# SwiGLU over 8192 rows: giving each partition a contiguous region of HBM of its own

## The chip, the cores and the metric

The kernel runs on one core of a Trainium2 chip. The metric is the device time of one execution in microseconds. Runs of one kernel are called fast or slow: a run over 1.5% above the fastest of the same kernel counts as slow, and ratios use fast runs alone.

## The reference

```python
x = np.random.randn(8192, 8192).astype(np.float32)

def reference(x):
    a, b = np.split(x, 2, axis=-1)
    silu_b = b / (1 + np.exp(-b))
    return a * silu_b
```

It reads 268.4 MB and writes 134.2 MB, and does two cheap operations per element.

## The kernel before

A tile is 128 partitions, each with two neighbouring rows of x (a "row pair", 64 KiB). Tile i takes row pairs 128 i to 128 i + 127, so a tile is one contiguous 8 MiB of HBM, and partition p lies 64 KiB after partition p - 1. Three buffers go round; SyncE issues loads, ScalarE issues stores, ScalarE computes silu and VectorE multiplies in place.

```python
    R = 2
    BUFS = 3
    xv = x.tensor.reshape([N // R, R * M]).ap()
    ov = out.tensor.reshape([N // R, R * half]).ap()
    ntiles = N // (P * R)          # 32
    ...
    def load(i, rows=None):
        ...
        nc.sync.dma_start(
            out=tiles[i][:, lo * M : hi * M], in_=xv[i * P : (i + 1) * P, lo * M : hi * M]
        )
    ...
    def store(i, c0=0, cw=R * half):
        (nc.scalar if i < last - 1 else nc.sync).dma_start(
            out=ov[i * P : (i + 1) * P, c0 : c0 + cw], in_=tiles[i][:, c0 : c0 + cw]
        )
```

Of the kernel before, what the change touches and what calls it, by code (L numbers as in the profile page):

```python
# [1 line left out]

# [4 lines left out]

_SILU = mybir.ActivationFunctionType.Silu


@with_exitstack
def kernel(
    ctx: ExitStack,
    tc: tile.TileContext,
    x: bass.AP,
    out: bass.AP,
):




    nc = tc.nc
    N, M = x.shape
    half = M // 2
    P = nc.NUM_PARTITIONS
    R = 2
    BUFS = 3

    xv = x.tensor.reshape([N // R, R * M]).ap()  # L30
    ov = out.tensor.reshape([N // R, R * half]).ap()
    ntiles = N // (P * R)
    last = ntiles - 1

    pool = ctx.enter_context(tc.tile_pool(name="sbuf", bufs=BUFS))
    ctx.enter_context(tc.manual_schedule())
    tiles = {}

    def load(i, rows=None):
        if i not in tiles:  # L40
            tiles[i] = pool.tile([P, R * M], x.dtype, name="xt")
        lo, hi = (0, R) if rows is None else rows
        nc.sync.dma_start(  # L43
            out=tiles[i][:, lo * M : hi * M], in_=xv[i * P : (i + 1) * P, lo * M : hi * M]
        )

    def swiglu(i, k, c0=0, cw=half):
        xt = tiles[i]
        b = xt[:, k * M + half + c0 : k * M + half + c0 + cw]
        nc.scalar.activation(out=b, in_=b, func=_SILU)  # L50
        nc.vector.tensor_mul(  # L51
            out=xt[:, k * half + c0 : k * half + c0 + cw],
            in0=xt[:, k * M + c0 : k * M + c0 + cw],
            in1=b,
        )

    def store(i, c0=0, cw=R * half):
        (nc.scalar if i < last - 1 else nc.sync).dma_start(
            out=ov[i * P : (i + 1) * P, c0 : c0 + cw], in_=tiles[i][:, c0 : c0 + cw]
        )  # L60

    for i in range(BUFS):
        load(i)
    for i in range(last):
        for k in range(R):
            swiglu(i, k)
        if i == last - 1:
            swiglu(last, 0)
        store(i)
        nxt = i + BUFS  # L70
        if nxt < last:
            load(nxt)
        elif nxt == last:
            load(last, (0, 1))
            load(last, (1, 2))

    store(last, 0, half)
    for c0 in range(0, half, half // 2):
        swiglu(last, 1, c0, half // 2)
    store(last, half, half)  # L80


# [1 line left out]
_INS = ['x']  # L84
_OUTS = [((8192, 4096), 'float32')]


# [23 lines left out]
```

## Time and profile before

| | before |
|---|---|
| time, median of 6 runs | 936.24 us (935.77 to 937.38) |
| span of the profiled run | 934.8 us |
| VectorE / ScalarE busy | 30% / 25% |
| packets on the DMA queues, share of 16 engines' span | 99.8% |
| steady rate | 434 GB/s |

A packet is one record of a DMA engine in the trace; a load is cut into 128 of them, one for the run of each partition. Three further lines of the page of before are of use later: the rate in 40 slices, and the issues with the median time from issue to landing at the end of the line.

```profile
GB/s 404 400 445 430 430 439 433 428 435 443 428 430 439 429 442 432 435 426 453 419 430 452 411 452 423 428 447 425 433 433 453 414 443 429 426 447 428 425 437 376
...
out_dram<-xt ACTq DMA_DIRECT2D x30, 4096.0 KB, 39.7
...
xt<-in_x_dram SPq DMA_DIRECT2D x31, 34.5
```

The reader is to see that from the third slice to the last but one the rate only wavers around 434 GB/s. A load of 8 MiB takes 34.5 us to land, and not the 19.3 us that eight packets per engine would take alone, because other transfers share the engines with it.

### The profile page before, as it was taken

The page shows a single profiled execution, that of the slowest core. Times are in us where ns is not written, and L with a number is a line of the kernel's source. Part 1 is how long each engine was busy: PE and PEld are TensorE (multiplying, and loading weights), DVE is VectorE, ACT ScalarE, POOL GpSimd, SP SyncE. Part 2 cuts the span into 40 slices and gives each one's busy share as a digit, 9 for nine tenths or more (in the row PEclk, how much of TensorE's full clock was granted, in tenths as well). Part 3 has the DMA queues.
Part 4 walks back from the last instruction along what each step waited for, and adds up shares of the span by engine and source line. Part 5 has one row for each costly group of instructions (what it writes and reads, how often), then busy time and mean ns, then how long its engine had stood idle before and what let it go on. Part 6 is the DMA issues. An engine that isn't in the chain of part 4 may idle for free.

```text
span 934.8 us, 367 instructions
## 1 busy us (share of the span) xinstructions
DVE 283.3 (30%) x65; ACT 229.4 (25%) x66; POOL 0.2 (0%) x4
## 2 busy tenths in 40 slices
DVE  0333312333123331133321333213332133331242
ACT  0223320233302333113331133311333203332041
POOL 0000000000000000000000000000000000000000
DMA  9999999999999999999999999999999999999998
GB/s 404 400 445 430 430 439 433 428 435 443 428 430 439 429 442 432 435 426 453 419 430 452 411 452 423 428 447 425 433 433 453 414 443 429 426 447 428 425 437 376
DMA packets 9506, 402.67 MB, mean 431 GB/s; under 512 B 1056, under 2 KB 1056, under 8 KB 1056
## 3 DMA queue, kind: packets, MB, share of 16 engines
q1 hardware_dynamic: 5184, 276.83, 68.6%
q10 hardware_dynamic: 4320, 125.83, 31.2%
q14 instruction: 2, 0.02, 0.0%
HBM read 268.44 MB, written 134.22 MB: 431 GB/s over the span
## 4 chain that ended last, share of the span: by engine, by line
DMA 84%; DVE 10%; ACT 4%; DVEq 0%; issue 0%; SPq 0%; ACTq 0%
DMA out_dram<-xt 42%; DMA xt<-in_x_dram 42%; DVE xt L51 10%; ACT xt L50 4%; DVEq L106 0%; SPq L43 0%; ACTq L50 0%; DVEq L51 0%
## 5 line engine op out<-in xcount | busy, mean ns | idle before, releaser
L51 DVE TENSOR_TENSOR xt<-xt 128x4096 f32<-128x4096 f32 (+1 forms) x65 | 283.3, 4359 | 637.7 <-ACT xt L50 634.5
L50 ACT ACTIVATE xt<-xt 128x4096 f32<-128x4096 f32 (+1 forms) x65 | 228.1, 3556 | 688.1 <-DMA xt<-in_x_dram 688.1
L50 ACT ACT_TABLE_LOAD x1 | 1.3, 1283 | 0.7 <-PEq L95 0.7
L95 POOL MEMSET const-bfloat16-1.0<- 128x1 bf16 x1 | 0.1, 103 | 0.0
L95 POOL MEMSET const-uint8-127<- 128x1 uint8 x1 | 0.1, 102 | 0.0
L95 POOL MEMSET const-float32-0.0<- 128x1 f32 x1 | 0.1, 100 | 0.2 <-issue 0.2
L95 POOL MEMSET const-float32-1.0<- 128x1 f32 x1 | 0.1, 99 | 0.0
## 6 DMA issues: line engine op xcount, KB each, us to landing
out_dram<-xt ACTq DMA_DIRECT2D x30, 4096.0 KB, 39.7
xt<-in_x_dram SPq DMA_DIRECT2D x2, 4096.0 KB, 27.1
out_dram<-xt SPq DMA_DIRECT2D x1, 4096.0 KB, 23.6
out_dram<-xt SPq DMA_DIRECT2D x2, 2048.0 KB, 14.5
xt<-in_x_dram SPq DMA_DIRECT2D x31, 34.5
```

The costliest lines, as they stand in the source:

```text
L50: nc.scalar.activation(out=b, in_=b, func=_SILU)
L51: nc.vector.tensor_mul(out=xt[:, k * half + c0 : k * half + c0 + cw], in0=xt[:, k * M + c0 : k * M + c0 + cw], in1=b,)
L95: nc = _bacc.Bacc("TRN2", target_bir_lowering=False, num_devices=1)
```

## The change

Its intent: each of 16 groups of 8 partitions works through a contiguous region of its own, 16 MiB of x and 8 MiB of out. Within a group every partition walks through its own 2 MiB of x, one row pair per tile.

```diff
-    xv = x.tensor.reshape([N // R, R * M]).ap()
-    ov = out.tensor.reshape([N // R, R * half]).ap()
     ntiles = N // (P * R)
+    G = 16
+    xv = x.rearrange("(e j i r) m -> i e j (r m)", i=ntiles, e=G, r=R)
+    ov = out.rearrange("(e j i r) m -> i e j (r m)", i=ntiles, e=G, r=R)
@@ load @@
-            out=tiles[i][:, lo * M : hi * M], in_=xv[i * P : (i + 1) * P, lo * M : hi * M]
+            out=tiles[i][:, lo * M : hi * M], in_=xv[i, :, :, lo * M : hi * M]
@@ store @@
-            out=ov[i * P : (i + 1) * P, c0 : c0 + cw], in_=tiles[i][:, c0 : c0 + cw]
+            out=ov[i, :, :, c0 : c0 + cw], in_=tiles[i][:, c0 : c0 + cw]
```

In the built program the pattern of a load is 128 runs of 16384 elements at a step of 524288 elements (2 MiB) instead of 16384 (64 KiB). The 16 x 8 of the source has folded into 128. This step from partition to partition is called the pitch below.

## The prediction

> **What bounds the kernel now.** I read the page's first two parts first, to see which engine is full:
>
> ```profile
> DVE 283.3 (30%) x65; ACT 229.4 (25%) x66; POOL 0.2 (0%) x4
> ...
> DMA  9999999999999999999999999999999999999998
> DMA packets 9506, 402.67 MB, mean 431 GB/s; under 512 B 1056, under 2 KB 1056, under 8 KB 1056
> ```
>
> VectorE and ScalarE are busy less than a third of the span of 934.8 us. The DMA row is at nine tenths or more in 39 of 40 slices. The small packets are 1056 semaphore writes of 4 bytes and carry nothing.
>
> Next the queues and the chain that ended last, to see what the transfers consist of and whether compute stands between them:
>
> ```profile
> q1 hardware_dynamic: 5184, 276.83, 68.6%
> q10 hardware_dynamic: 4320, 125.83, 31.2%
> ...
> DMA 84%; DVE 10%; ACT 4%; DVEq 0%; issue 0%; SPq 0%; ACTq 0%
> ```
>
> The two shares add to 99.8% of what 16 engines could do in the span, so there is practically no gap. The 14% of DVE and ACT in the chain are not gaps of the DMA either: while one tile is computed, the other two buffers of the ring load or store. The busy time by window confirms this; its columns are the window, its length, the busy time of DVE, ACT and POOL with counts, PEclk, the DMA share and GB/s:
>
> ```profile
> 0.00:12.00 12.00, 0.00 (x0) 1.28 (x1) 0.20 (x4) 1.00 0.86 350
> 12.00:46.00 34.00, 8.85 (x2) 7.12 (x2) 0.00 (x0) 1.00 1.03 427
> 46.00:75.00 29.00, 8.85 (x2) 7.12 (x2) 0.00 (x0) 1.00 1.00 434
> ...
> 400.00:487.00 87.00, 25.93 (x7) 20.75 (x7) 0.00 (x0) 1.00 1.00 434
> ...
> 900.00:935.00 35.00, 9.51 (x4) 7.33 (x3) 0.00 (x0) 1.00 0.91 393
> ```
>
> In the steady part the share is 1.00 and the rate 434 GB/s. Finally I read the single packet records of the trace. Of the 3968 packets of 65,536 bytes, median and ninth decile are both 2418 ns (27.1 GB/s per engine; times 16 that is 433.7 GB/s). The 3840 packets of 32,768 bytes on the store queue take 1213 ns, with a maximum of 1221 ns. Such constancy says that nothing behind the engines, HBM in particular, ever holds a packet up: the engine sets its own pace. All long packets but two fall into the first 55 us, where the queues start (3.0 to 3.5 us for the first ones, up to 4.1 us where stores first join loads).
>
> So the floor of this program is 402.65 MB / 434 GB/s = 928 us. The span is 935 us: 7 us of start and tail are all that could be won with the same bytes.
>
> **What the Trainium skill says.**
> 1. "DMA: Bandwidth & Descriptors", section "Where 436 GB/s comes from", puts the ceiling of 16 engines at 435.2 GB/s. The trace agrees: 434 in every steady window. "HBM Reference", section "Specifications (TRN2)", gives 716 GB/s for the memory that two cores share, so with one core running HBM has room above the 434 as long as its parts are evenly loaded. The equal packet times are consistent with that.
> 2. "DMA: Bandwidth & Descriptors", section "Latency and other measured facts", row "HBM row pitch at large powers of two", bears directly on the change. Copies of 128 partitions x 16 KiB between HBM tensors reached, per direction, 207 GB/s at a pitch of 512 KiB from partition to partition, 164 at 2 MiB, 103 at 4 and 8 MiB, and 214 again at 4 MiB padded by 4 KiB. The page calls channel aliasing of streams in lockstep an inference. The trace of before cannot test it: its pitches are only 64 KiB (loads) and 32 KiB (stores), and it shows no slow steady state there.
> 3. The same page, section "The descriptor swizzle", has 16 engines with 8 partitions each. The trace fits: an 8 MiB load is 128 packets of 64 KiB, eight per engine, 8 x 2.418 = 19.3 us.
>
> **The change part by part.** It removes and adds no instruction. In the built program the order on every engine is the same: 31 loads of 128 x 16384 elements, two half loads, 33 stores, 65 activations, 65 multiplications, the same three buffers and waits. The SBUF side is identical. The split of 128 partitions into 16 groups of 8 folds back into one step, because eight steps of 2 MiB make exactly 16 MiB. What is left is this:
> - A load's partition step in x goes from 64 KiB to 2 MiB; the run within a partition stays 64 KiB (32 KiB in the halves of the last tile).
> - A store's partition step in out goes from 32 KiB to 1 MiB; the run stays 32 KiB.
> - From tile to tile the loads move 64 KiB instead of 8 MiB.
>
> A. Descriptors and issue: same counts and sizes, hence 0 us.
> B. ScalarE and VectorE: same shapes, 65 x 3.51 us and 65 x 4.36 us, both under a third of the span; 0 us.
> C. Locality: every partition walks through its own 2 MiB. This could only save something if HBM held the engines up now, and constant 2418 ns say it does not. At most a few us at the start; I count 0.
> D. Pitch, loads: the 16 engines now start at addresses that differ by multiples of 8 or 16 MiB, all advancing from the same offset. The page's 2 MiB figure is 164 / 214 = 0.77 of full. Estimate: 434 x 0.77 = 333 GB/s, so 268.4 MB take 806 us instead of 618 us: +188 us.
> E. Pitch, stores: 1 MiB lies between the page's 512 KiB (207 / 214 = 0.97) and 2 MiB (0.77). With 0.86 the rate is 373 GB/s and 134.2 MB take 360 us instead of 309 us: +51 us.
>
> The DMA is the path that sets the end, so D and E lie wholly on it: 936 + 188 + 51 = 1175 us if the page's ratios carry over in full. They may not. The page's copies both read and write HBM in each packet, with both sides at the bad pitch; here each packet has HBM on one side and SBUF on the other. Its row was 16 KiB and here it is 64 or 32 KiB, so an engine running 20 us ahead is on another partition and others may slip past it. And one core at 434 GB/s leaves headroom below 716. I take about 60% of the 239 us: 936 + 144 = 1080 us.
>
> **Rivals.**
> 1. The pitch does nothing: the headroom absorbs uneven load, or the engines fall out of step and stay so. For: in the first 4 us of before the sixteen first packets start within 0.8 us of each other, take up to 3.47 us, and from the second packet on nearly all take 2418 ns, with starts spread over only 0.6 us. A small offset is enough there. Against: those were 64 KiB steps, where different address bits differ. Result: 933 to 940 us.
> 2. Locality is worth something, and the larger regions help. For: a change of this intent. Against: the engines are at their own pace, floor 928 us. Result: 930 us at best, which is less than 2%.
> 3. Both sides alias in full: all 402.65 MB at 333 GB/s is 1209 us plus 7 for start and tail, 1216 us. The limit could even apply per direction: 268.4 MB at 164 GB/s would be 1637 us, which I hold for unlikely because then the loads would have to run at less than half of an engine's pace.
> 4. Waits take over: if loads slow down and stores do not, the loads' queue is the longer one, and ScalarE waits for it as it does now (688 us of its 935 us waiting). Three buffers are then just as short as before; no new bound, but the idle of both engines grows with the span.
>
> **Range and chances.** The outcomes have two humps: near 936 (rivals 1 and 2, some 38%) and a broad one from 1000 to 1240 (D and E in part or whole, some 60%). The range from 932 to 1240 takes in both; the rest lies above. The point, 1080, is a compromise weighted to the second hump. Faster by over 2% would need under 918 us, below the floor of 928: 1%. Within 2%: 38%. Slower: 61%.
>
> **What would show it.** If D holds, the 64 KiB packets of the load queue take more than 2418 ns throughout and scatter (3150 ns at the page's ratio), the steady windows keep a DMA share near 1.00 but fall from 434 to between 330 and 400 GB/s, and ACT's wait for loads grows. E shows in 32 KiB packets of the store queue longer than 1213 ns, less so than the loads (1.16 times against 1.30 times). A and B hold if packet counts and the means of 3.5 and 4.4 us stand. Rival 1 shows as 2418 and 1213 ns unchanged. The prediction is wrong in its main step if packet times are unchanged, or if only one of the two queues slows while the other keeps its time; and it is wrong in size if packets take over 1.4 times as long.

## The result, and the profile after

The changed kernel takes 997.83 us (median of 6 runs, 995.75 to 1004.92) against 936.24 us: slower, ratio 1.0668, 95% interval 1.0635 to 1.0701. A ratio here is the mean time of one kernel's fast runs over that of the other's fast runs in the same rounds, so it is not quite the ratio of the medians quoted. The result is correct.

From the page of the changed kernel, the lines that answer to those of before:

```profile
DVE 283.3 (28%) x65; ACT 229.4 (23%) x66; POOL 0.2 (0%) x4
...
DMA  9999999999999999999999999999999999999995
GB/s 350 374 386 405 413 425 421 414 428 404 416 422 407 429 416 426 411 421 416 409 433 414 409 401 412 417 405 407 404 392 389 388 421 403 392 405 411 404 418 251
DMA packets 9506, 402.67 MB, mean 404 GB/s; under 512 B 1056, under 2 KB 1056, under 8 KB 1056
...
q1 hardware_dynamic: 5184, 276.83, 68.9%
q10 hardware_dynamic: 4320, 125.83, 29.7%
...
DMA 82%; DVE 10%; ACT 4%; another core or an unknown queue 1%; issue 0%; DVEq 0%; ACTq 0%; SPq 0%
...
out_dram<-xt ACTq DMA_DIRECT2D x30, 4096.0 KB, 40.8
...
xt<-in_x_dram SPq DMA_DIRECT2D x31, 38.4
```

Packet counts, bytes and compute times are those of before. The engines are still full (98.6% of 16 spans), but they move 404 GB/s instead of 431. So the packets themselves became longer. Loads land 3.9 us later, stores 1.1 us. (The 1% of "another core or an unknown queue" is mostly one wait of 13.5 us near the start that the profile could not assign.)

The windows of the changed kernel (columns as in the prediction: window, length, DVE, ACT and POOL busy with counts, PEclk, DMA share, GB/s):

```profile
0.00:12.00 12.00, 0.00 (x0) 1.28 (x1) 0.20 (x4) 1.00 0.97 350
12.00:46.00 34.00, 8.85 (x2) 7.12 (x2) 0.00 (x0) 1.00 0.98 369
46.00:75.00 29.00, 8.85 (x2) 7.12 (x2) 0.00 (x0) 1.00 1.01 386
75.00:104.00 29.00, 8.85 (x2) 7.12 (x2) 0.00 (x0) 1.00 0.98 398
104.00:133.00 29.00, 8.85 (x2) 7.12 (x2) 0.00 (x0) 1.00 1.01 424
400.00:487.00 87.00, 23.11 (x6) 20.08 (x6) 0.00 (x0) 1.00 1.01 418
487.00:574.00 87.00, 24.36 (x6) 17.04 (x6) 0.00 (x0) 1.00 1.00 416
870.00:900.00 30.00, 8.85 (x2) 7.12 (x2) 0.00 (x0) 1.00 1.00 405
900.00:935.00 35.00, 8.85 (x2) 7.12 (x2) 0.00 (x0) 1.00 0.99 408
935.00:997.00 62.00, 17.77 (x5) 14.45 (x5) 0.00 (x0) 1.00 0.81 341
```

Worst is the start, where the sixteen engines begin together: 369 GB/s where before had 427. By 104 us most of the loss is gone, but it does not heal: 416 to 424 GB/s against 434 follow, and in the second half the rate falls again (396 GB/s from 700 to 800 us, 405 and 408 in the windows above). The last window is new: the share is only 0.81, so 0.19 x 62 = 12 us of engine time are idle there. Over the whole run 1.34% of 996.1 us are idle, against 0.22% of 934.8 us before: 11 us more. The engines no longer finish together: from the first to the last of the 16 landing records of one transfer, the median is 16.8 us (before: 2.5 us), and the longest 30.7 us.

The packet records of the trace give the sum. Durations in ns (median, ninth decile, mean):

| packets | before | after |
|---|---|---|
| 64 KiB loads (3968) | 2418, 2418, 2427 | 2418, 3069, 2604 |
| 32 KiB stores on ScalarE's queue (3840) | 1213, 1213, 1213 | 1213, 1213, 1233 |

Per engine there are 3968 / 16 = 248 such load packets and 240 such stores: 248 x 0.1776 us = 44 us and 240 x 0.0198 us = 5 us. The half loads and the stores of the last tiles add 1 us. With the 11 us of added idle time, that is 61 us, as much as the difference between the spans. 55% of the load packets still take exactly the 2418 ns of before; the loss sits in the 40% that take over 2450 ns.

### The profile page after: what moved, and what is told of

Same layout as the page of the kernel before. It is cut to its first block, busy times and chain, and to the rows that moved or that the text cites. A ratio compares the mean times of both kernels' runs of the same rounds, so it can differ in the third digit from the quotient of the medians.

```text
span 996.1 us, 367 instructions
## 1 busy us (share of the span) xinstructions
DVE 283.3 (28%) x65; ACT 229.4 (23%) x66; POOL 0.2 (0%) x4
## 4 chain that ended last, share of the span: by engine, by line
DMA 82%; DVE 10%; ACT 4%; another core or an unknown queue 1%; issue 0%; DVEq 0%; ACTq 0%; SPq 0%
DMA out_dram<-xt 41%; DMA xt<-in_x_dram 41%; DVE xt L53 10%; ACT xt L52 4%; DVEq L108 0%; SPq L45 0%; ACTq L60 0%; ACTq L52 0%; DVEq L53 0%
## 5 line engine op out<-in xcount | busy, mean ns | idle before, releaser
L53 DVE TENSOR_TENSOR xt<-xt 128x4096 f32<-128x4096 f32 (+1 forms) x65 | 283.3, 4359 | 699.0 <-ACT xt L52 695.8
L52 ACT ACTIVATE xt<-xt 128x4096 f32<-128x4096 f32 (+1 forms) x65 | 228.1, 3556 | 749.4 <-DMA xt<-in_x_dram 749.4
```

The lines of the kernel that those rows point to most:

```text
L52: nc.scalar.activation(out=b, in_=b, func=_SILU)
L53: nc.vector.tensor_mul(out=xt[:, k * half + c0 : k * half + c0 + cw], in0=xt[:, k * M + c0 : k * M + c0 + cw], in1=b,)
```

## The experiments

Two theories stood at the start. **Alignment**: engines that run together read addresses that differ by multiples of a large power of two and collide in HBM. **Distance**: each packet pays for jumping to a region far from the last one, whatever the exact step. A third question was whether loads or stores lose the time. Fifteen runs were made. Those called "wrong on purpose" read or write other places than the reference asks.

### Loads alone, stores alone

`loads_far`, the pattern of the loads changed, of the stores not:

```diff
+    xv = x.rearrange("(p i r) m -> i p (r m)", r=R, p=P)
+    ov = out.rearrange("(i p r) m -> i p (r m)", r=R, p=P)
```

> Loads at the changed pitch (2 MiB from partition to partition), stores at the old one; result wrong on purpose. Alignment theory (streams of different engines that advance at addresses equal but for large powers of two collide in HBM) and distance theory (each packet pays for jumping to a far region) both put the loss where the long packets are: the trace of the changed kernel has 64 KiB load packets at a mean of 2604 ns against 2427, store packets at 1233 against 1213, so some 44 of 49 us per engine. Both expect 980 to 1000 us, with store packets back at 1213 ns. A rival that stores cause the loss (writes that disturb reads) expects 936 to 950 us.

Measured: 973.38 us (969.09 to 974.36), ratio 1.0388. Load packets have a mean of 2528 ns. The store packets did not go back to 1213 ns but stayed at 1232, though their own addresses are the old ones: far loads hold up stores too. The time is also below the expected 980 us; whether the stores' own pitch has a part is for the next run.

`stores_far`, the other way round:

```diff
+    xv = x.rearrange("(i p r) m -> i p (r m)", r=R, p=P)
+    ov = out.rearrange("(p i r) m -> i p (r m)", r=R, p=P)
```

> Stores at the changed pitch (1 MiB), loads at the old one; result wrong on purpose. If only loads matter: 935 to 945 us, load packets 2418 to 2430 ns. If stores at a far pitch disturb the loads: 955 us or more, with long load packets though the loads' own pitch is the old one.

Measured: 943.64, 948.77 and 953.53 us in the fast runs, ratio 1.0132, and one slow run of 980.00. This lies between the two expectations. Stores alone cost some 12 us (6 to 18 by the ratio's interval of 1.0070 to 1.0193), and in the profiled run the load packets have a mean of 2455 ns although their pitch is the old one. Of 936.2 us, 3.88% is 36 us and 1.32% is 12 us, together 49; the changed kernel loses 6.68%, 62 us. The other 14 us (with the same uncertainty of 6) arise only when both are far. Why single runs of this kernel scatter by 4% stays open.

### A small offset in the pitch

`pad4k`: as the changed kernel, but the loads' step is 2 MiB less 4 KiB (wrong).

```diff
+    xv = bass.AP(tensor=x.tensor, offset=0, ap=[[R * M, ntiles], [ntiles * R * M - 1024, P], [1, R * M]])
+    ov = out.rearrange("(p i r) m -> i p (r m)", r=R, p=P)
```

> As the changed kernel, but the loads' pitch is 2 MiB less 4 KiB (rows cut wrongly, result wrong on purpose); same packets, same distances between streams but for 0.2%. Alignment theory: back to 936 to 950 us, load packets near 2420 ns. Distance theory: stays at 985 to 1005 us.

Measured: fast runs of 947.24 to 951.50 us, ratio 1.0145, and a slow one of 980.56 us, which was the profiled one, so the expected packet times were not tested in a fast run. The fast runs equal those of `stores_far` (ratio 1.0132), as if the loads' part were gone and the stores' part left. That fits alignment, but the stores blurred it, and in the slow run the padded loads still have packets with a mean of 2535 ns, which stays unexplained; hence two runs with the stores as before. `lpad4k` has this load pattern, `lpad256` has 64 elements in place of 1024:

```diff
-    xv = bass.AP(tensor=x.tensor, offset=0, ap=[[R * M, ntiles], [ntiles * R * M, P], [1, R * M]])
+    xv = bass.AP(tensor=x.tensor, offset=0, ap=[[R * M, ntiles], [ntiles * R * M - 1024, P], [1, R * M]])
```

> Loads at 2 MiB less 4 KiB, stores as in the kernel before (result wrong on purpose). To be set against 973 us for loads at exactly 2 MiB with the same stores. Alignment theory: 935 to 942 us. Distance theory: 968 to 978 us.

Measured: 936.80 us (936.34 to 937.61), ratio 1.0007, interval 0.9992 to 1.0022. Load packets: 2418 ns at the ninth decile, a mean of 2428, as before. An offset of 0.2% of the pitch removes the whole loss of `loads_far` (973.38 us). Distance falls here for the loads.

> The same with 256 bytes instead of 4 KiB (result wrong on purpose). If what collides are places in HBM coarser than some KiB, 256 bytes do not help: 965 to 978 us. If any offset breaks the collision: 935 to 945 us.

Measured: 943.96, 945.28, 950.20 and 956.69 us in the four fast runs, and slow runs of 959.05 and 996.66 us. The ratio of 1.0089 fits the two fastest runs alone; the mean of the four is 1.014 times the 936.2 us of before. Neither expectation holds for the runs as a whole: 256 bytes help in most runs and not in all. How fine the colliding places are stays open.

### The same intent at a pitch that is no power of two

`pitch31` gives the right result: each partition has a contiguous region of 31 row pairs, and the last tile takes the 128 pairs left over.

```diff
+    K = 31
+    x31 = x[: P * K * R, :].rearrange("(p k r) m -> k p (r m)", k=K, r=R)
+    o31 = out[: P * K * R, :].rearrange("(p k r) m -> k p (r m)", k=K, r=R)
+    xz = x[P * K * R :, :].rearrange("(p r) m -> p (r m)", r=R)
+    oz = out[P * K * R :, :].rearrange("(p r) m -> p (r m)", r=R)
@@ load @@
+            out=tiles[i][:, lo * M : hi * M], in_=(x31[i] if i < K else xz)[:, lo * M : hi * M]
@@ store @@
+            out=(o31[i] if i < K else oz)[:, c0 : c0 + cw], in_=tiles[i][:, c0 : c0 + cw]
```

> Right result. Each partition keeps its own contiguous region, of 31 row pairs instead of 32; the last tile takes the 128 pairs left over. Pitch 1984 KiB for loads and 992 KiB for stores: as far apart as in the changed kernel, but not a power of two. Alignment theory: 935 to 943 us, load packets at 2418 to 2435 ns. Distance theory (far jumps cost, whatever the pitch): 985 to 1000 us.

Measured: 936.51 us (936.20 to 936.84, six runs), ratio 1.0002, interval 0.9988 to 1.0016. Its windows:

```profile
12.00:46.00 34.00, 8.85 (x2) 7.12 (x2) 0.00 (x0) 1.00 1.02 426
46.00:75.00 29.00, 8.85 (x2) 7.12 (x2) 0.00 (x0) 1.00 1.00 434
...
400.00:487.00 87.00, 25.83 (x7) 20.65 (x7) 0.00 (x0) 1.00 1.00 433
```

Against 369, 386 and 418 GB/s of the changed kernel, 426, 434 and 433 are the rates of before. Regions are as far apart as in the changed kernel to within 3%, for loads and stores alike. So the exact step is shown to be the cause, as alignment has it, and distance has fallen; that the place of the collision is HBM itself is argued. The run also shows that contiguity per partition is worth nothing here: it ties with before. No version was found that beats before, and none could win more than the 7 us above the floor that the prediction works out.

### The size of the pitch

`pitch512k` and `pitch1m` give the right result; a partition's contiguous stretch is K = 8 or K = 16 row pairs, and the stretches follow one after the other.

```diff
+    K = 8
+    x4 = x.rearrange("(o p k r) m -> o k p (r m)", p=P, k=K, r=R)
+    o4 = out.rearrange("(o p k r) m -> o k p (r m)", p=P, k=K, r=R)
@@ load @@
+            out=tiles[i][:, lo * M : hi * M], in_=x4[i // K, i % K, :, lo * M : hi * M]
@@ store @@
+            out=o4[i // K, i % K, :, c0 : c0 + cw], in_=tiles[i][:, c0 : c0 + cw]
```

> Right result. As the changed kernel, but each partition's contiguous stretch is 8 row pairs: pitch 512 KiB for loads, 256 KiB for stores, four stretches one after the other. Alignment by address: small or no loss, 936 to 950 us. If any pitch beyond the contiguous 64 KiB costs the same: near 998 us.

> Right result. The same with 16 row pairs: loads at a pitch of 1 MiB, stores at 512 KiB. If the loss grows with the power of two: between the run at 512 KiB and 998 us, some 945 to 980 us. If the loss has a threshold at 2 MiB: 936 to 945 us.

Measured: 941.28 us (940.31 to 949.23, ratio 1.0072) and 963.07 us (959.50 to 964.76, ratio 1.0281).

| loads' / stores' pitch | time, us | ratio | mean 64 KiB load, ns |
|---|---|---|---|
| 64 / 32 KiB (before) | 936 | 1 | 2427 |
| 512 / 256 KiB | 941 | 1.0072 | 2432 |
| 1 MiB / 512 KiB | 963 | 1.0281 | 2516 |
| 2 / 1 MiB (the change) | 998 | 1.0668 | 2604 |

Among these four, the loss grows with the power of two and does not start at 2 MiB.

### Two runs that tested something else than meant

To tell distance between engines from jumps within an engine, `eng_apart` kept the groups 16 MiB apart but put the 8 partitions of a group side by side, and `eng_near` did the reverse.

```diff
+    xv = x.rearrange("(e i j r) m -> i e j (r m)", r=R, e=16, j=8)     # eng_apart; out likewise
+    xv = x.rearrange("(j i e r) m -> i e j (r m)", r=R, e=16, j=8)     # eng_near; out likewise
```

> Right result. The 16 groups of 8 partitions keep their own 16 MiB region, but within a group the 8 partitions of a tile are next to each other (64 KiB), so each group reads 512 KiB in one run per tile. Alignment between engines: the groups are still 16 MiB apart and in step, so 980 to 1060 us. Distance within an engine (jump of 2 MiB from one packet to the next): back to 936 to 945 us.

> Right result. The mirror of the run with 16 apart groups: the same three-step access pattern of 16 x 8 x 64 KiB, but now the 16 groups lie 64 KiB apart within one tile and the 8 partitions of a group 32 MiB apart. If the loss of 1.66 times came from address distance between engines that run together: back to 936 to 970 us. If it came from how a 16 x 8 pattern is split over the engines[...]: again about 1550 us, with load packets near 4600 ns.

Measured: 1552.62 us (1548.88 to 1567.10, ratio 1.6612) and 1534.54 us (1475.46 to 1545.11; by the 1.5% rule only the fastest of the four is a fast run, so there is no ratio). Both give the right result and both miss what alignment or distance expected. Unlike in the changed kernel, these patterns do not fold: a load is 16 x 8 runs against 128 partitions. `split_local` has such a pattern in the loads at practically the addresses of before (a gap of one row pair between groups; wrong), with the stores as before:

```diff
+    xv = bass.AP(tensor=x.tensor, offset=0, ap=[[127 * R * M, ntiles], [9 * R * M, 16], [R * M, 8], [1, R * M]])
```

> Loads as a pattern of 16 x 8 runs with only 64 KiB between neighbours and 128 KiB between groups (a gap of one row pair, so that the pattern does not fold into 128 steps), stores as before; result wrong on purpose. Addresses are practically those of the kernel before. If the 1.6 times of the two 16 x 8 runs came from the pattern's split over engines: 1300 to 1560 us, load packets near 4500 ns. If from addresses: 935 to 945 us.

Measured: 1532.49 us (1472.07 to 1544.60; again only the fastest run is fast, 1.57 times before, and the profiled one, 1536.62 us, is slow). Its rate in 40 slices:

```profile
GB/s 219 217 258 271 273 259 261 271 267 270 264 266 260 272 270 269 266 260 261 268 271 255 268 259 268 274 254 273 258 266 269 260 260 272 265 266 263 257 257 259
```

In the first slice loads run alone (the first store is issued at 57 us), and 219 GB/s is half of 434. The 64 KiB packets of the run have a mean of 4569 ns in place of 2427; in the fast profiled run of `eng_apart` it is 4658 ns. A factor near two is far outside the scatter of 5%, so it is the form of the pattern and not the addresses. What in the hardware this form slows is not shown. The two runs say nothing on alignment.

### Why the loss was smaller than the page's ratios

The ratios in the prediction come from copies with runs of 16 KiB and with HBM on both sides (the Trainium skill, "DMA: Bandwidth & Descriptors", row "HBM row pitch at large powers of two"; "the page" below). Four runs vary these. `before_q4` and `after_q4` are the two kernels with every load cut into transfers of 16 KiB per partition:

```diff
-        nc.sync.dma_start(
-            out=tiles[i][:, lo * M : hi * M], in_=xv[i * P : (i + 1) * P, lo * M : hi * M]
-        )
+        q = half
+        for c in range(lo * M, hi * M, q):
+            nc.sync.dma_start(out=tiles[i][:, c : c + q], in_=xv[i * P : (i + 1) * P, c : c + q])
```

> Right result. The kernel before with each load in pieces of 16 KiB per partition. Control for the next run; 930 to 950 us.

> Right result. The changed kernel with each load in pieces of 16 KiB per partition. If my estimate was too high because the runs here are longer than the 16 KiB of the page's copies: clearly over the changed kernel's 998 us, 1050 us or more. If run length does not matter: 990 to 1005 us, the control's difference added.

Measured: 950.45 us (949.26 to 950.77) and 1151.61 us (1147.02 to 1157.19), both correct. By their ratios to before, 1.0147 and 1.23, the pitch now costs 1.23 / 1.0147 = 1.21 times, or 201 us instead of 62. Windows of `after_q4`:

```profile
46.00:75.00 29.00, 4.43 (x1) 5.34 (x2) 0.00 (x0) 1.00 1.00 321
...
400.00:487.00 87.00, 23.15 (x6) 18.08 (x5) 0.00 (x0) 1.00 1.00 356
487.00:574.00 87.00, 17.70 (x4) 15.81 (x5) 0.00 (x0) 1.00 1.00 348
```

The DMA share is 1.00 and the rate 321 to 356 GB/s: the same full engines, with slower packets. The store packets, whose size and addresses are those of the changed kernel, now have a mean of 1551 ns against 1233.

`copy_near` and `copy_far` do no computing; they copy the left halves of x's rows into out, 128 x 16 KiB at a time (wrong):

```diff
+    xv = x.rearrange("(p k) m -> k p m", p=P)        # copy_far;  copy_near: "(k p) m -> k p m"
+    ov = out.rearrange("(p k) m -> k p m", p=P)
+    for k in range(N // P):
+        (nc.sync if k % 2 == 0 else nc.scalar).dma_start(out=ov[k], in_=xv[k][:, :half])
```

> No computing, result wrong on purpose: the left halves of x's rows go from HBM to out in HBM, 134 MB, in 64 transfers of 128 x 16 KiB at a pitch of 32 KiB (x) and 16 KiB (out). Control for the next run. At the page's full rate of 207 to 214 GB/s in each direction: 627 to 648 us.

> The same copy at the changed kernel's pitches, 2 MiB in x and 1 MiB in out. If the page's loss holds for copies with HBM on both sides: the ratio to the control is 1.15 to 1.30 (page: 1.31 at 2 MiB, 1.03 at 512 KiB). If this chip loses less than the page says: a ratio under 1.10, near the 1.067 of the changed kernel.

Measured: 420.88 us (418.33 to 423.46) and 592.96 us (590.45 to 595.57), a quotient of medians of 1.41. The loss in copies is real on this chip, and larger than the page's 1.31 at 2 MiB; the control is much faster than expected (134.2 MB / 420.88 us = 319 GB/s in each direction). It is no undisturbed baseline, though: its 16 KiB packets on SyncE's queue have a mean of 825 ns and a ninth decile of 1188, where the 16 KiB loads of `before_q4` have a mean of 618.

So the order is 1.07 with long runs and HBM on one side, 1.21 with 16 KiB loads and HBM on one side, and 1.41 with 16 KiB runs and HBM on both sides. Cutting the loads alone turns 62 us into 201; it shortens the run and also changes the order in which a partition's 64 KiB are read, which no run here separates. From 1.21 to 1.41 several things change at once (both sides in HBM, stores of 16 KiB too, no computing), so what HBM on one side is worth is not shown. Why long runs protect is argued only: within one 16 KiB transfer all engines are in the same small range of offsets, while with 64 KiB they can spread over four times as much and fall out of step, as the recovery in the first 104 us suggests. Being out of step is no full cure: the rate fell again, to 396 GB/s, between 700 and 800 us, when the landings of one transfer were up to 30 us apart.

## Why the prediction was right or wrong

- **What bounds the kernel**: right. The same engines bound it after, at 98.6% of 16 spans, and constant packet times of before were the proper baseline: the whole loss but 11 us of added idle time is packets longer than 2418 and 1213 ns.
- **A and B** (issue, compute): right. Packet counts are equal, VectorE is busy 283.3 us in both and ScalarE 229.4 us.
- **C** (locality is worth 0): right; `pitch31` has far-apart contiguous regions and ties with before.
- **D** (pitch, loads): the mechanism is right, as `lpad4k` and `pitch31` show. The size was far off: +188 us in full, about 113 at the 60% taken; measured alone, 36 us.
- **E** (pitch, stores): right that it is smaller than D; 51 us in full, about 31 at 60%, measured alone 12 us with much scatter.
- **The time**: 998 us falls between the two humps, just under the second one (1000 to 1240 us). The direction was right for the reason given; the point, 1080 us, added 144 us where 62 came.
- **The step that failed** is "I take about 60% of the 239 us". The loss was 62 us, 26% of 239. The prediction itself named the longer row as a reason for a discount, but sized the discount from nothing. With the page's own 16 KiB in the loads the loss was 201 us, 84% of the sum; so with 64 KiB runs two thirds of that loss are gone, and this is the term that was mis-sized. That 84% is so near to the whole is partly luck: the page's ratio is from copies, and the copies here lost more than it says (1.41 against 1.31). The headroom of a single core is the same in both runs and can't explain the difference between them; neither it nor HBM on one side only was varied by itself. A slip in the same place: "an engine running 20 us ahead is on another partition" is too strict, since one packet is one partition's run; 2.4 us ahead is enough.
- **A term that was missing**: loads and stores are not independent. Together they lose 14 us more than the sum of both alone, and each makes the other's packets longer. A second missing term is the added idle time, 11 us, most of it at the ragged end.
- **Rival 1** fell, yet its observation was half right: engines get out of step (landings 16.8 us apart) and the rate recovers from 369 to 418 GB/s, but not to 434. **Rivals 2 and 3** fell. **Rival 4** is as told: ScalarE's wait for loads grew from 688.1 to 749.4 us and caused nothing.
- **The signs**: scatter above 2418 ns came, but "throughout" was wrong, since the median stayed. The mean load packet grew 1.07 times instead of 1.30, the mean store packet 1.02 times instead of 1.16. A steady rate between 330 and 400 GB/s was mostly wrong: in windows of 29 to 100 us from 104 to 935 us it was 404 to 424, and below 400 only from 700 to 800 us (396).

## What to carry to other kernels

When a kernel is bound by DMA engines whose packets all take the same time, as here, a better layout in HBM has little to win (`pitch31` ties), but the address pattern can still slow it: look at the step between partitions, and avoid large powers of two (31 row pairs instead of 32 held in six of six runs, 4 KiB of padding in the loads in four of four, but not in every run where the stores kept their power of two) or keep the tile contiguous. If such a step can't be avoided, keep the run per partition in one transfer long (62 us lost with 64 KiB loads, 201 with 16 KiB). Check in the built program that a pattern split into groups folds back to 128 steps, since a pattern of 16 x 8 ran the loads at half rate.

## What the Trainium skill lacked or had wrong

- "DMA: Bandwidth & Descriptors", row on HBM row pitch: it gives one run length, 16 KiB. Here the pitch cost 1.21 times with loads cut into 16 KiB, 1.067 with 64 KiB loads in the same kernel. It also has no figure for 1 MiB: here 1.028 with 64 KiB loads.
- The same row calls 214 GB/s per direction the full rate of its HBM to HBM copies. Here 319 GB/s were measured at a pitch of 32 and 16 KiB, and 226 at 2 MiB and 1 MiB, where the page has 164 at 2 MiB.
- The same row says that a padding of 192 bytes does not help at a pitch of 4 MiB. Here, at 2 MiB, 256 bytes less in the loads' pitch gave 944 to 959 us in five runs and 997 in one, against 973 without. These are other sizes, so this adds to the row and does not refute it.
- The same row leaves channel aliasing an inference. The runs agree that alignment and not distance is the cause (936.5 us at 1984 KiB, 998 us at 2048 KiB) but do not show which part of HBM it is, nor that it is HBM.
- "DMA: Bandwidth & Descriptors", "Rules for kernel authors", asks for an outermost dimension that is a multiple of 16, ideally the 128 partitions. No page says that 16 x 8 on the HBM side against 128 partitions runs loads at half rate: 219 GB/s, 64 KiB packets of 4569 ns (both from a slow run of `split_local`), and 1472 us for the kernel in its fast run.
